# Two post-norm layers on one core: six weight rows instead of four are left to the second token block, the layer norms lose their GpSimd halves, and a layer starts 1024 columns wide

## Chip, cores and metric

The kernel runs on one core of one Trainium2 chip. The metric is the device time of one execution in microseconds (us), the median of three runs. The profile shows one execution of its own, with a span from its first to its last instruction.

## What is computed

A sequence of 256 tokens with 1024 features, in float32, goes through four pre-norm layers (an FFN, a mixer and an FFN each; the mixers are Gated DeltaNet, stick-breaking attention, sparse attention and Gated DeltaNet again), an RMS norm, and two post-norm ("deepnorm") layers. The change is about the two last layers:

```python
for i in range(4):
    x = x + 0.5 * swiglu(rmsnorm(x), ...)          # a0..a3
    x = x + mixer_i(rmsnorm(x))                     # m0 gdn, m1 stick, m2 dsa, m3 gdn
    x = x + 0.5 * swiglu(rmsnorm(x), ...)          # c0..c3
x = rmsnorm(x, final_norm)
for l in range(2):                                  # s0, s1
    h = x @ w_in_2[l]                               # 7696 columns: three branches and their gates
    m = sum(gate_b * (branch_b(h) @ w_branch_2[l, b]) for b in range(3)) @ w_out_2[l]
    x = layer_norm(ALPHA * x + m, ln1_g, ln1_b)     # ALPHA = 4 ** 0.25
    f = relu(x @ w_ff1[l]) ** 2 @ w_ff2[l]          # 4096 wide
    x = layer_norm(ALPHA * x + f, ln2_g, ln2_b)
```

In Gated DeltaNet (`gdn`) each head inverts a unit triangular system of 64 by 64 for each chunk of 64 tokens.

## The kernel before

All activations stay on chip; 503 MB of weights stream through. `fetch` brings 1 MB into a tile `st`; ScalarE (ACT) casts it into the high halves `wh` (L319), and VectorE (DVE) computes the low halves `wl` = `st` - `wh` (L324), so that each product takes three TensorE (PE) matmuls: high by high, high by low, low by high. `wh` and `wl` have WB buffers each. PSUM has eight banks of 512 columns: four with the tag `acc`, two `mm` and two `tr`.

SBUF work tiles come from SLOTS slots of 512 columns. `t()` takes the slot that has been free the longest, `free()` puts one at the end of the line, both while the program is traced. So the number of slots decides which earlier tile a new one takes over from, and whose readers it has to wait for.

The instructions are traced in Python, and a scheduler then gives each engine one fixed order, by priorities (the order of tracing, moved by `rank`) and its own estimates. On the chip each engine follows its order and stops at the first instruction whose inputs or buffers aren't ready.

**The joints in s0 and s1.** A layer norm ends a group of matmuls, `accumulate`, into four `acc` banks (two token blocks t by two halves c of the columns). The last call finishes block 0 over its weight rows and then block 1, so that `deepnorm` can normalize block 0 meanwhile. `deepnorm` forms ALPHA * x + acc (L1316), takes statistics (L1318, L1321), 1/sqrt (`rsqrt1`, L361 to L370), and scales (L1327 on ACT, L1328 on GpSimd, L1329 and L1336 on DVE). For the first half of block 1, ACT copies the bank (L1311) and GpSimd (POOL) does the multiply and the sum (L1312, L1313). `next` puts two of the next weights' `wl` on GpSimd and holds the following four behind the end of block 1's norm, through the list `holds`. Then `xT` transposes x on PE (L418) and splits it (ACT L422, DVE L424): block 0 first; `finish()` does block 1. `cols512(first=True)` multiplies block 0 by 512 columns of weights (L499 to L502) and calls `finish()` in the middle of it. There are three such joints: in s0 from ln1 to its FFN, from s0's ln2 to s1, and in s1 from ln1 to its FFN. An FFN starts with `square` (relu squared: ACT L1592, DVE L1593).

**The solve in `gdn`** (stages m0 and m3, two groups G of heads each: `solve(0)`, `solve(1)`) doubles the solved diagonal blocks in five levels: 32 matmuls of 64 by 64 (L772) into an `acc` bank, a predicated copy on DVE (L773), 32 matmuls (L777), a transpose on DVE (L779) and a copy on ACT (L780), after which the next L772 can start. Between these the scheduler places other PE work, above all projections (`proj_feat`, L588 to L590) into the `mm` banks; each such bank is read out by L644 in `qkv`, into a slot (`c0`).

Of the kernel before, what the change touches and what calls it, by code (L numbers as in the profile page):

```python
# [18 lines left out]
P = 128  # L19
S = 256  # L20
# [5 lines left out]
SLOTS = 57  # L26
ST = 3
WB = 6
# [40 lines left out]
# 16 columns, and zeros up to 128  # L69
# [36 lines left out]
def second_blocks(i, l):  # L106
    w = i["w_in_2"][l]
    z = lambda c: [pack(w[:512, c : c + 512]), pack(w[512:, c : c + 512])]
    out = z(1024) + [pack(padded(w[:, 2048:2064]))]
    for c in (1536, 0, 512, 3088, 3600, 4112, 2064, 2576, 4624, 5136, 5648, 6160, 6672, 7184):  # L110
# [82 lines left out]
# [P, n, S], two blocks of features to a tile  # L193
# [10 lines left out]
class Build:  # L204
# [19 lines left out]
    # loads a set of functions for ScalarE, behind an instruction  # L224
# [6 lines left out]
    # Exp and Ln from one set  # L231
# [3 lines left out]
    # instructions traced here compete as if traced at point p  # L235
# [6 lines left out]
    # a goes behind b on their engine  # L242
# [13 lines left out]
    # a few columns of SBUF  # L256
# [3 lines left out]
    # [P, 512] of PSUM  # L260
# [3 lines left out]
    # up to 512 columns of SBUF, in the slot that has been free the longest  # L264
# [22 lines left out]
    # loads the next block of the weight stream, with x(i) behind each of its n parts  # L287
# [12 lines left out]
    # next block of the weight stream, [P, a, b], as a (h, l) for each of its a rows:  # L300
    # exact float32r halves, w == h + l
# [37 lines left out]
    # y = 1/sqrt(v), elementwise on [P, n]  # L339
# [16 lines left out]
    # y = 1/sqrt(v) for one column: a Newton step with constants for this first guess, then a cubic step  # L356
# [16 lines left out]
    # halves of (x * g)^T, [P (feature), NK, S], of x in blocks of features; g: the stage that has the gain  # L373
# [9 lines left out]
    # sums of x^2 of every token: two columns  # L383
# [15 lines left out]
    # 1/sqrt(mean(x^2) + eps) of every token: two columns, and along the free axis  # L399
# [9 lines left out]
    # halves of x^T of token blocks. The first block is taken as soon as it is there; finish() takes the second.  # L409
# [21 lines left out]
    # r of every token along the free axis, the same on every partition  # L431
# [10 lines left out]
    # acc[t][c] += pairs of feature blocks @ their rows of the next weights;  # L442
    # at the end the blocks of tokens are finished one after the other
    def accumulate(self, acc, pairs, first, last):
        ws = [self.weights(2, 1024) for _ in pairs]
        n = len(pairs)
        order = [(i, a, t, c) for i in range(n) for a in range(2) for t in range(2) for c in range(2)]
        if last:
            self.mark = None
            order = [(i, a, t, c) for t in range(2) for c in range(2) for i in range(n) for a in range(2)]  # L450
        for i, a, t, c in order:
            if last and t and self.mark is None:
                self.mark = self.tc.cur_priority
            (hT, lT), (wh, wl) = pairs[i], ws[i][a]
            q = slice(t * P, t * P + P)
            s = slice(c * 512, c * 512 + 512)
            self.mm3(acc[t][c], hT[:, a, q], lT[:, a, q], wh[:, s], wl[:, s], first and i == 0 and a == 0, last and i == n - 1 and a == 1)
# [27 lines left out]
    # products of both token blocks with the next 512 columns of weights, in step or one after the other  # L485
    # (the first ones of a stage, while the second block of tokens is still on its way)
    def cols512(self, X, banks, first=False):
        XH, XL = X
        w = self.w2()
        mm = self.nc.tensor.matmul  # L490
        if first:
            for t in range(2):
                q = slice(t * P, t * P + P)
                for g in range(0, NK, 4):
                    if (t, g) == (0, 4):
                        self.finish()
                    for k in range(g, g + 4):
                        wh, wl = w[k]
                        mm(banks[t], XH[:, k, q], wh, start=k == 0, stop=False)  # L499
                        mm(banks[t], XH[:, k, q], wl, start=False, stop=False)  # L500
                    for k in range(g, g + 4):
                        mm(banks[t], XL[:, k, q], w[k][0], start=False, stop=k == NK - 1)  # L502
                if t == 0:
                    self.mid = self.tc.cur_priority
            return
# [7 lines left out]
    # x += 0.5 * swiglu(rmsnorm(x))  # L513
# [36 lines left out]
    # x += heads @ w_out, by features  # L550
# [8 lines left out]
    # [128 features, S] products with the next 512 columns of weights, two blocks of features to a bank  # L559
# [16 lines left out]
    # [tok, n] products of a token block  # L576
# [5 lines left out]
    # [128 features, S] products, features f*128.. of the block  # L582
# [9 lines left out]
    # two heads of proj_feat in a bank  # L592
# [8 lines left out]
    def gdn(self, x, st):  # L601
# [33 lines left out]
        # silu of the convolution of a kind (q, k, v) of a group: [feature, 2 heads, tok] twice  # L635
# [30 lines left out]
        # squared norms of the heads of [tok, 4 * 128]  # L666
# [8 lines left out]
        # beta and decay of each token and head  # L675
# [31 lines left out]
        # decay from token j to token i, [i, j] for j <= i  # L707
# [14 lines left out]
        # U = T^T of T = (I - am)^-1, am the strict part of the system, negated (its diagonal is never used); rows scaled: 1/rk T rk  # L722
        def solve(G):
# [38 lines left out]
            # doubling of the diagonal blocks, up to 64: both of them on their half of the partitions  # L762
# [38 lines left out]
        def scan(G):  # L801
# [35 lines left out]
            # scale of the queries: P^-1/2 / norm  # L837
# [19 lines left out]
        # gates and normalizes the heads; their halves, transposed  # L857
# [40 lines left out]
    # halves of a [feature, 2, S] bank  # L898
# [19 lines left out]
    # stick-breaking attention; keys on partitions, queries along the free axis.  # L918
    # z, sp and att hold (key block 0, queries 0..255) and (key block 1, queries 128..255)
# [56 lines left out]
    # rotary embedding of the first r of every group of n columns: [P, groups, n] -> out  # L976
# [16 lines left out]
    # attention weights of a head: (queries 0..127, keys 0..127) and (queries 128..255, keys 0..255);  # L993
    # mask is added to the scores
# [20 lines left out]
    # out [d, S] = the weights p of a head, times its values in two blocks of tokens  # L1015
# [11 lines left out]
    # halves of transposes of [tok, n * 128] columns: [P, n, S], scaled by g along the features  # L1027
# [12 lines left out]
    def dsa(self, x, st):  # L1040
# [6 lines left out]
        # cq 384, k_rope 32, k_idx 64, w_idx 8; and c_kv 256  # L1047
# [19 lines left out]
        # 1/rms of c_q, c_kv and k_idx; c_q and c_kv are scaled by theirs after the products with them  # L1067
# [11 lines left out]
        # cos and sin times 1/rms of c_q: [P, 2, 2, 16] and [P, 2, 2, 8]  # L1079
# [29 lines left out]
        # index keys and queries, [feature, tok]; the keys lie twice on the partitions  # L1109
# [20 lines left out]
        # scores  # L1130
# [22 lines left out]
        # heads: the 96 plain features first, then the 32 rotated ones  # L1153
# [37 lines left out]
        # the largest 64 scores of each query  # L1191
# [32 lines left out]
    # a [1, n] input on every partition, in tiles of 512 columns  # L1224
# [9 lines left out]
    # x * gain * r of all tokens, in blocks of tokens, [t][c]  # L1234
# [16 lines left out]
    # the rotations and the causal mask of the last two stages  # L1251
# [8 lines left out]
    # cos and sin of positions * inv, [P, 2, 16] each  # L1260
# [34 lines left out]
    # the weights of the next stage wait while block t is finished, by instruction z  # L1295
    def next(self, t, z):
        self.holds += [[None] * 2 + ["gpsimd"] * 2, [z] * 4][t]

    # x = layer norm of ALPHA * x + acc, one block of tokens and then the other
    def deepnorm(self, x, acc, gname, bname):  # L1300
# [377 lines left out]
```

## Time and profile before

| | |
|---|---|
| time, median of 3 runs | 3035.79 us (3034.38 to 3035.9) |
| span of the profiled execution | 3030.8 us |
| mean granted clock of TensorE | 0.994 |
| PE busy | 2986.9 us, 99% of the span |
| DVE, ACT, POOL busy | 65%, 51%, 6% |
| waits of PE by the chain of semaphores: largest, L418 for L1336 | 10.0 us in 6 waits |

The profiled execution has no time of its own besides its span; the median run is 5.0 us longer than that span, which is what lies before the first and behind the last instruction. A difference is added to either. PE is busy nearly all the time, so what counts is where it isn't, and where its clock isn't full.

### The profile page before, as it was taken

How to read it: one execution, taken by the hardware profiler on the slowest of the kernel's cores; microseconds unless marked ns; L12 is line 12 of the kernel's file. 1: busy time of each engine (PE TensorE's matmuls, PEld its weight loads, DVE VectorE, ACT ScalarE, POOL GpSimd, SP SyncE). 2: the span in 40 equal slices, each digit the busy share in tenths (PEclk: the TensorE clock that was granted, in tenths of full speed). 3: DMA queues.
4: the chain of work that ended last, by engine and by line, in shares of the span. 5: the costliest groups of instructions: out<-in, count | busy, mean ns of one | idle time of the engine just before them, and what ended most of it. 6: DMA issues, size and time to landing. Idle time of an engine off the chain costs nothing.

```text
span 3030.8 us, 56638 instructions
## 1 busy us (share of the span) xinstructions
PE 2986.9 (99%) x23672; PEld 2843.2 (94%) x23672; DVE 1956.4 (65%) x3013; ACT 1542.2 (51%) x2887; POOL 188.6 (6%) x191
## 2 busy tenths in 40 slices
PE   9999999999999999999999999999999999999998
PEld 9998999999899999879999999999889898889897
DVE  6569865755565565676565598855766756665755
ACT  5455554544554454565454465544554554554553
POOL 1011000000110000210000020000000101000100
PEclk9999999999999999999999999999999999999999
DMA  6442355555445555425555542454455465355453
GB/s 248 181 174 99 112 182 188 185 183 181 153 166 183 181 184 192 153 98 191 186 181 183 172 142 83 175 187 164 164 176 186 172 203 175 139 184 179 174 201 112
DMA packets 73617, 513.07 MB, mean 169 GB/s; under 512 B 8414, under 2 KB 8430, under 8 KB 13456
## 3 DMA queue, kind: packets, MB, share of 16 engines
q1 hardware_dynamic: 70992, 502.50, 46.8%
q0 software_dynamic: 2080, 6.43, 0.8%
q8 instruction: 185, 3.03, 0.4%
q14 instruction: 72, 0.59, 0.1%
q10 hardware_dynamic: 288, 0.52, 0.0%
HBM read 508.37 MB, written 1.05 MB: 168 GB/s over the span
## 4 chain that ended last, share of the span: by engine, by line
PE 54%; DVE 3%; ACT 1%; issue 1%; POOL 0%; DVEq 0%; POOLq 0%; ACTq 0%
PE mm L571 5%; PE mm L573 5%; PE mm L572 5%; PE acc L336 3%; PE acc L335 3%; PE acc L337 3%; PE acc L478 3%; PE acc L477 3%; PE acc L479 3%; PE tr L571 2%; PE tr L573 2%; PE tr L572 2%; PE mm L337 1%; PE mm L335 1%; PE mm L336 1%; PE mm L590 1%
## 5 line engine op out<-in xcount | busy, mean ns | idle before, releaser
L319 ACT CAST wh<-st 128x512 fp32r<-128x512 f32 x1909 | 1093.2, 617 | 1118.8 <-issue 428.6
L324 DVE TENSOR_TENSOR wl<-st,wh 128x1024 fp32r<-128x1024 f32 (+1 forms) x946 | 1155.5, 1228 | 774.3 <-ACT wh L319 771.2
L571 PE MATMUL mm<-s,wh 128*128 128x256 f32 x2240 | 633.5, 283 | 7.1 <-ACT wh L319 7.1
L573 PE MATMUL mm<-s,wl 128*128 128x256 f32 x2240 | 633.1, 283 | 0.1
L572 PE MATMUL mm<-s,wh 128*128 128x256 f32 x2240 | 632.3, 282 | 0.0
L478 PE MATMUL acc<-s,wh 128*128 128x256 f32 x1664 | 468.7, 282 | 0.0
L479 PE MATMUL acc<-s,wl 128*128 128x256 f32 x1664 | 467.5, 282 | 0.0
L477 PE MATMUL acc<-s,wh 128*128 128x256 f32 x1664 | 465.9, 282 | 0.0
L571 PEld LDWEIGHTS mm<-s,wh 128*128 128x128 f32 x2240 | 424.7, 190 | 8.1 <-ACT wh L319 7.1
L572 PEld LDWEIGHTS mm<-s,wh 128*128 128x128 f32 x2240 | 424.6, 190 | 0.7
L573 PEld LDWEIGHTS mm<-s,wl 128*128 128x128 f32 x2240 | 424.1, 189 | 0.3 <-DVE wl L324 0.3
L572 PE MATMUL tr<-s,wh 128*128 128x256 f32 x1280 | 361.6, 282 | 0.0
L571 PE MATMUL tr<-s,wh 128*128 128x256 f32 x1280 | 361.6, 282 | 0.0
L573 PE MATMUL tr<-s,wl 128*128 128x256 f32 x1280 | 360.9, 282 | 0.0
L478 PEld LDWEIGHTS acc<-s,wh 128*128 128x128 f32 x1664 | 314.0, 189 | 1.7 <-DVE s L905 1.3
L479 PEld LDWEIGHTS acc<-s,wl 128*128 128x128 f32 x1664 | 313.4, 189 | 0.0
L477 PEld LDWEIGHTS acc<-s,wh 128*128 128x128 f32 x1664 | 312.6, 189 | 0.1
L572 PEld LDWEIGHTS tr<-s,wh 128*128 128x128 f32 x1280 | 242.1, 189 | 0.0
L571 PEld LDWEIGHTS tr<-s,wh 128*128 128x128 f32 x1280 | 242.0, 189 | 0.0
L573 PEld LDWEIGHTS tr<-s,wl 128*128 128x128 f32 x1280 | 241.8, 189 | 0.0
L335 PE MATMUL acc<-wh,s 128*128 128x512 f32 (+1 forms) x410 | 159.8, 390 | 1.3 <-DVE s L1002 1.0
L337 PE MATMUL acc<-wh,s 128*128 128x512 f32 (+1 forms) x410 | 160.6, 392 | 0.0
(490 smaller groups left out, 4590.4 us busy)
## 6 DMA issues: line engine op xcount, KB each, us to landing
st<-w SPq DMA_DIRECT2D x468, 1024.0 KB, 4.9
st<-w SPq DMA_DIRECT2D x4, 768.0 KB, 4.2
st<-w SPq DMA_DIRECT2D x8, 256.0 KB, 6.0
st<-w SPq DMA_DIRECT2D x4, 512.0 KB, 3.5
s<-s_ln_g POOLq DMA_DIRECT2D x8, 256.0 KB, 3.7
s<-s_ln_b POOLq DMA_DIRECT2D x8, 256.0 KB, 4.5
st<-w SPq DMA_DIRECT2D x2, 976.0 KB, 4.9
s<-x SPq DMA_DIRECT2D x4, 256.0 KB, 5.7
```

The source lines that it names most:

```text
L319: nc.scalar.copy(h[:, o : min(m, o + 512)], st[:, i * b + o : i * b + min(m, o + 512)])
L324: z = e.tensor_tensor(l[:, c], st[:, i * b + c.start : i * b + c.stop], h[:, c].bitcast(F32), ALU.subtract)
L335: mm(out, xh, wh, start=start, stop=False)
L336: mm(out, xh, wl, start=False, stop=False)
L337: mm(out, xl, wh, start=False, stop=stop)
L477: mm(out, wh[:, s], h, start=begin and f == 0, stop=False, skip_group_check=True)
L478: mm(out, wh[:, s], l, start=False, stop=False, skip_group_check=True)
L479: mm(out, wl[:, s], h, start=False, stop=end, skip_group_check=True)
L571: mm(out, wh[:, s], XH[:, k, :], start=k == 0 and f % 2 == 0, stop=False, skip_group_check=True)
L572: mm(out, wh[:, s], XL[:, k, :], start=False, stop=False, skip_group_check=True)
L573: mm(out, wl[:, s], XH[:, k, :], start=False, stop=k == NK - 1, skip_group_check=True)
L590: mm(out, wl[:, s], XH[:, k, :], start=False, stop=k == NK - 1, skip_group_check=True)
```

## The change

The slots go from 57 to 45, the weight buffers from 6 to 9. The last `accumulate` leaves six rows (`apart=6`) of eight to be done block by block, where it was four of four; for that it takes all four pairs of blocks at once (in the FFN the seventh chunk waits for the eighth). In `deepnorm` the first half of block 1 is done on DVE as the others are, `next` goes, and with it the holds: the scheduler places the `wl` of the next weights. A new function `ahead` takes the place of `cols512(first=True)`: the FFN starts with 512 columns as before, s1 with 1024 (banks and `gb`), block 0 first. The weight blocks of s0 and s1 are reordered to suit. Lines that only lose a comment are left out of the diff. Line numbers shift: in `gdn` by two (L772 is now L774, L777 L779, L779 L781, L644 L646), in `deepnorm` by nine (L1316 is L1307, L1318 L1309, L1336 L1327), in `square` L1593 is L1584.

```diff
-SLOTS = 57
+SLOTS = 45
 ST = 3
-WB = 6
+WB = 9
...
-    def accumulate(self, acc, pairs, first, last):
-        ws = [self.weights(2, 1024) for _ in pairs]
-        n = len(pairs)
-        order = [(i, a, t, c) for i in range(n) for a in range(2) for t in range(2) for c in range(2)]
-        if last:
-            self.mark = None
-            order = [(i, a, t, c) for t in range(2) for c in range(2) for i in range(n) for a in range(2)]
-        for i, a, t, c in order:
-            if last and t and self.mark is None:
+    def accumulate(self, acc, pairs, first, last, apart=6):
+        rows = [(z[0][:, a, :], z[1][:, a, :], *w) for z in pairs for a, w in enumerate(self.weights(2, 1024))]
+        n = len(rows)
+        m = n - apart if last else n
+        order = [(i, t, c) for i in range(m) for t in range(2) for c in range(2)]
+        order += [(i, t, c) for t in range(2) for c in range(2) for i in range(m, n)]
+        for z, (i, t, c) in enumerate(order):
+            if last and z == len(order) - 2 * apart:
                 self.mark = self.tc.cur_priority
...
+    def ahead(self, X, pairs):
+        XH, XL = X
+        mm = self.nc.tensor.matmul
+        w = [self.w2() for _ in pairs]
+        end = (0, len(pairs) - 1, 4)
+        for t, i, g in [(t, i, g) for t in range(2) for i in range(len(pairs)) for g in range(0, NK, 4)]:
+            q, out = slice(t * P, t * P + P), pairs[i][t]
+            if (t, i, g) == end:
+                self.finish()
+            for k in range(g, g + 4):
+                wh, wl = w[i][k]
+                mm(out, XH[:, k, q], wh, start=k == 0, stop=False)
+                mm(out, XH[:, k, q], wl, start=False, stop=False)
+            for k in range(g, g + 4):
+                mm(out, XL[:, k, q], w[i][k][0], start=False, stop=k == NK - 1)
...
-    def next(self, t, z):
-        self.holds += [[None] * 2 + ["gpsimd"] * 2, [z] * 4][t]
...
-                if not end and (t, c) == (1, 0):
-                    y = self.t(512)
-                    A.copy(y, acc[t][c])
-                    G_.tensor_scalar(x[t][c], x[t][c], ALPHA, None, ALU.mult)
-                    G_.tensor_tensor(x[t][c], x[t][c], y, ALU.add)
-                    self.free(y)
-                else:
-                    z = V.scalar_tensor_tensor(x[t][c], x[t][c], ALPHA, acc[t][c], ALU.mult, ALU.add)
-                    self.behind(z, None if end else done)
+                z = V.scalar_tensor_tensor(x[t][c], x[t][c], ALPHA, acc[t][c], ALU.mult, ALU.add)
+                self.behind(z, None if end else done)
...
-            self.next(t, done)
...
-        self.cols512(X, banks, not start)
+        gb = [self.bank("acc") for _ in range(2)]
         if start:
+            self.cols512(X, banks)
             ps = self.sums(x)
+            p = self.tc.cur_priority
+            self.cols512(X, gb)
+        else:
+            self.ahead(X, [banks, gb])
...
-        self.cols512(X, b2, True)
+        self.ahead(X, [b2])
...
-            self.accumulate(acc, prev, ch == 0, ch == 7)
+            if ch == 6:
+                held = prev
+            else:
+                self.accumulate(acc, held + prev if ch == 7 else prev, ch == 0, ch == 7)
```

The scheduler's orders show three places. The first is PE in `solve(0)` of m0, the second and third levels of the doubling (L772 and L777; the projections are L588 to L590). Before:

```order
L772 MATMUL acc_2933<-s_361_2804,s_332_2629 64x64 x8
L772 MATMUL acc_2933<-s_361_2804,s_335_2636 64x64 x8
L590 MATMUL mm_3664<-s_267_2280,wl_3585 128x256
L588 MATMUL mm_3664<-s_267_2280,wh_3584 128x256
L589 MATMUL mm_3664<-s_271_2284,wh_3584 128x256
L590 MATMUL mm_3664<-s_267_2280,wl_3585 128x256
L590 MATMUL mm_3603<-s_268_2281,wl_3592 128x256
L588 MATMUL mm_3603<-s_268_2281,wh_3591 128x256
L589 MATMUL mm_3603<-s_272_2285,wh_3591 128x256
L590 MATMUL mm_3603<-s_268_2281,wl_3592 128x256
L588 MATMUL mm_3603<-s_269_2282,wh_3596 128x256
L777 MATMUL acc_2951<-s_383_2893,s_360_2803 64x64 x16
```

Now (L774 and L779 are the solve's; L755 are transposes for `solve(1)`; the three levels after the second stand as bare):

```order
L779 MATMUL acc_2913<-s_382_2892,s_360_2803 64x64 x16
L755 MATMUL tr_3191<-s_357_2742 128x128 x2
L774 MATMUL acc_2933<-s_361_2804,s_332_2629 64x64 x8
L774 MATMUL acc_2933<-s_361_2804,s_335_2636 64x64 x8
L779 MATMUL acc_2951<-s_383_2893,s_360_2803 64x64 x16
L774 MATMUL acc_2971<-s_361_2804,s_332_2629 64x64 x8
L774 MATMUL acc_2971<-s_361_2804,s_335_2636 64x64 x8
L779 MATMUL acc_2989<-s_382_2892,s_360_2803 64x64 x16
```

Nine projections stood between this L772 and its L777, and 21, 8, 15, 10 and 11 in the places that follow; now the first projection stands behind the fifth level's L774. The order of m3 has the same piece.

The second place is DVE in the same stretch, with buffer numbers (`s37_445` is tile 445 in slot 37; `nm` is `s43_383`, which L779 `acc_391` reads). L644, now L646, reads out a projection's bank. Before:

```order
L324 TENSOR_TENSOR wl_454_3585<-st_450_3577,wh_453_3584 128x1024
L352 SCALAR_TENSOR_TENSOR rsy8_371_2830<-rsa8_372_2831,rsj8_370_2829 128x8
L644 TENSOR_TENSOR s37_445_3456<-mm_446_3457,s33_315_2570 128x512
L350 SCALAR_TENSOR_TENSOR rsa8_372_2831<-rsy8_371_2830 128x8
L351 TENSOR_TENSOR rsa8_372_2831<-rsa8_372_2831,nv_362_2806 128x8
```

Now:

```order
L781 STREAM_TRANSPOSE s23_360_2803<-acc_389_2989 128x512
L775 COPY_PREDICATED s43_383_2893<-prm_72,acc_390_3009 128x512
L781 STREAM_TRANSPOSE s23_360_2803<-acc_391_3027 128x512
L646 TENSOR_TENSOR s43_445_3456<-mm_446_3457,s12_315_2570 128x512
L775 COPY_PREDICATED s42_382_2892<-prm_72,acc_392_3047 128x512
L652 SCALAR_TENSOR_TENSOR s42_444_3455<-s43_445_3456,prm_72,s42_444_3455 128x255
```

The read-out of bank `mm_446` stood ahead of the solve's first level; it now takes the slot of a tile of the solve and stands behind the solve's fourth level.

The third place is DVE at the joint in s0 from ln1 to the FFN: the norm of token block 1. Before (behind the last row two L1336 and then `square`'s L1593 follow):

```order
L1318 BN_STATS lnst_27585<-s_3343_25042 128x6
L1321 BN_AGGR lnmv_27593<-lnst_27585 128x2
L1323 TENSOR_SCALAR nmu_27595<-lnmv_27593 128x1
L1324 TENSOR_SCALAR lnmv_27593<-lnmv_27593 128x1
L1329 SCALAR_TENSOR_TENSOR s_3342_25041<-s_3342_25041,lnmv_27593,s_3748_27546 128x512
L361 TENSOR_SCALAR r1i_27598<-lnmv_27593 128x1
L362 TENSOR_SCALAR r1j_27599<-r1i_27598 128x1
L364 TENSOR_SCALAR r1a_27601<-r1j_27599,lnmv_27593 128x1
```

Now (ahead of it stand L1307 and one more `wl`; behind it the rest of `rsqrt1` and two L1327):

```order
L1309 BN_STATS lnst_27585<-s_3343_25042 128x6
L324 TENSOR_TENSOR wl_27754<-st_27746,wh_27753 128x1024
L1312 BN_AGGR lnmv_27590<-lnst_27585 128x2
L324 TENSOR_TENSOR wl_27761<-st_27758,wh_27760 128x1024
L1314 TENSOR_SCALAR nmu_27592<-lnmv_27590 128x1
L1315 TENSOR_SCALAR lnmv_27590<-lnmv_27590 128x1
L1320 SCALAR_TENSOR_TENSOR s_3342_25041<-s_3342_25041,lnmv_27590,s_3748_27546 128x512
L361 TENSOR_SCALAR r1i_27595<-lnmv_27590 128x1
L324 TENSOR_TENSOR wl_27766<-st_27758,wh_27765 128x1024
L362 TENSOR_SCALAR r1j_27596<-r1i_27595 128x1
L1584 SCALAR_TENSOR_TENSOR s_3801_27739<-mm_27646,s_3800_27738 128x512
L324 TENSOR_TENSOR wl_27905<-st_27902,wh_27904 128x1024
```

Five `wl` now stand inside this norm, and `square`'s L1584 (between its neighbours L362 and L364) has moved ahead of the norm's end. On PE the transposes of block 1 stand directly behind the 24 matmuls of block 0.

## Rows read from the trace of the kernel before

**Rows 1.** The page: span, and busy time of each engine.
```profile
span 3030.8 us, 56638 instructions
PE 2986.9 (99%) x23672; PEld 2843.2 (94%) x23672; DVE 1956.4 (65%) x3013; ACT 1542.2 (51%) x2887; POOL 188.6 (6%) x191
```

**Rows 2.** PE's waits: total us, times, longest us.
```profile
PE tr L418 <- DVE s L1336: 10.0, 6, 4.3
PE mm L571 <- ACT wh L319: 7.1, 1, 7.1
```

**Rows 3.** Busy time in two stretches of m0: window, length, each engine, granted clock.
```profile
260.00:320.00 60.00, 59.67 (x945) 54.35 (x944) 51.33 (x118) 27.87 (x57) 6.62 (x8) 1.00 0.23 83
320.00:360.00 40.00, 39.98 (x322) 36.99 (x321) 33.91 (x84) 21.55 (x43) 0.00 (x0) 1.00 0.24 90
```

**Rows 4.** Timeline, all engines, one level of `solve(1)` in m0: start, us, engine, instruction.
```profile
307.79 0.28 PE L777 MATMUL acc<-s,s 64*64 64x64 f32 x4
...
308.12 0.72 DVE L779 STREAM_TRANSPOSE s<-acc 128x512 f32<-128x512 f32 x1 [1.36 <-PE acc L777]
...
308.92 0.59 ACT L780 COPY s<-acc 128x512 f32<-128x512 f32 x1 [4.45 <-DVE s L779]
...
309.41 0.28 PE L589 MATMUL mm<-s,wh 128*128 128x256 f32 x1
...
309.52 0.28 PE L590 MATMUL mm<-s,wl 128*128 128x256 f32 x1
...
309.74 1.15 PE L772 MATMUL acc<-s,s 64*64 64x64 f32 x32
...
310.81 0.38 PE L588 MATMUL mm<-s,wh 128*128 128x256 f32 x1
...
311.00 0.74 DVE L773 COPY_PREDICATED s<-prm,acc 128x512 f32<-128x512 int32 x1 [2.17 <-PE acc L772]
...
311.95 1.15 PE L777 MATMUL acc<-s,s 64*64 64x64 f32 x32
```

**Rows 5.** PE alone in four stretches: window, length, PE busy, granted clock, DMA.
```profile
1325.90:1329.80 3.90, 1.92 (x9) 1.00 0.10 40
1329.80:1333.20 3.40, 3.40 (x15) 0.51 0.64 198
...
2381.65:2384.60 2.95, 2.95 (x9) 0.51 0.00 0
2571.80:2575.70 3.90, 3.87 (x11) 0.50 0.74 271
```

**Rows 6.** Timeline of PE at the joint in s0, with the idle time before.
```profile
2378.89 0.63 PE L418 MATMUL tr<-ident,s 128*128 128x128 f32 x4 [0.59 <-DVE s L1336]
...
2381.65 1.09 PE L418 MATMUL tr<-ident,s 128*128 128x128 f32 x4 [1.89 <-DVE s L1336]
...
2384.62 0.39 PE L500 MATMUL mm<-wl,s 128*128 128x512 f32 x1
...
2385.08 0.40 PE L500 MATMUL mm<-wl,s 128*128 128x512 f32 x1
```

**Rows 7.** Timeline of DVE at the same joint.
```profile
2377.55 3.95 DVE L1336 SCALAR_TENSOR_TENSOR s<-s,r1z,s 128x512 f32<-128x512 f32 x2
...
2384.13 0.68 DVE L1318 BATCH_NORM_STATS2 lnst<-s 128x6 f32<-128x512 f32 x1
...
2388.00 1.42 DVE L1336 SCALAR_TENSOR_TENSOR s<-s,r1z,s 128x512 f32<-128x512 f32 x2
2389.87 0.69 DVE L1593 SCALAR_TENSOR_TENSOR s<-mm,s 128x512 f32<-128x512 f32 x1 [0.46 <-ACT s L1592]
```

**Rows 8.** Timeline of POOL at the same joint.
```profile
2378.15 5.58 POOL L324 TENSOR_TENSOR wl<-st,wh 128x1024 fp32r<-128x1024 f32 x2
```

**Rows 9.** Timeline of PE at the joint from s0 to s1.
```profile
2571.83 1.12 PE L418 MATMUL tr<-ident,s 128*128 128x128 f32 x4 [4.32 <-DVE s L1336]
```

**Rows 10.** The page's group of DVE's `wl`: busy us, mean ns, idle before.
```profile
L324 DVE TENSOR_TENSOR wl<-st,wh 128x1024 fp32r<-128x1024 f32 (+1 forms) x946 | 1155.5, 1228 | 774.3 <-ACT wh L319 771.2
```

More of the change, by code (lines that the diff above doesn't have):

```diff
@@ L108, in second_blocks @@
     z = lambda c: [pack(w[:512, c : c + 512]), pack(w[512:, c : c + 512])]
-    out = z(1024) + [pack(padded(w[:, 2048:2064]))]
-    for c in (1536, 0, 512, 3088, 3600, 4112, 2064, 2576, 4624, 5136, 5648, 6160, 6672, 7184):
+    out = z(1024) + z(1536) + [pack(padded(w[:, 2048:2064]))]
+    for c in (0, 512, 3088, 3600, 4112, 2064, 2576, 4624, 5136, 5648, 6160, 6672, 7184):
         out += z(c)
@@ L440, in along @@
         return rb
-    def accumulate(self, acc, pairs, first, last):
-        ws = [self.weights(2, 1024) for _ in pairs]
-        n = len(pairs)
-        order = [(i, a, t, c) for i in range(n) for a in range(2) for t in range(2) for c in range(2)]
-        if last:
-            self.mark = None
-            order = [(i, a, t, c) for t in range(2) for c in range(2) for i in range(n) for a in range(2)]
-        for i, a, t, c in order:
-            if last and t and self.mark is None:
+    def accumulate(self, acc, pairs, first, last, apart=6):
[6 more added lines that the diff above has]
+            if last and z == len(order) - 2 * apart:
                 self.mark = self.tc.cur_priority
-            (hT, lT), (wh, wl) = pairs[i], ws[i][a]
+            hT, lT, wh, wl = rows[i]
             q = slice(t * P, t * P + P)
             s = slice(c * 512, c * 512 + 512)
-            self.mm3(acc[t][c], hT[:, a, q], lT[:, a, q], wh[:, s], wl[:, s], first and i == 0 and a == 0, last and i == n - 1 and a == 1)
+            self.mm3(acc[t][c], hT[:, q], lT[:, q], wh[:, s], wl[:, s], first and i == 0, last and i == n - 1)
         self.free(*pairs)
@@ L483, in accs, with cols512 @@
         return [[self.bank("acc") for c in range(2)] for t in range(2)]
-    def cols512(self, X, banks, first=False):
+    def cols512(self, X, banks):
         XH, XL = X
         w = self.w2()
[L490 to L505, printed above, removed]
         for k in range(NK):
@@ L511, in cols512 @@
                 self.mm3(banks[t], XH[:, k, q], XL[:, k, q], *w[k], k == 0, k == NK - 1)
+    def ahead(self, X, pairs):
[13 more added lines that the diff above has]
+                mm(out, XL[:, k, q], w[i][k][0], start=False, stop=k == NK - 1)
+            if (t, i, g) == end:
+                self.mid = self.tc.cur_priority
     def ffn(self, x, st):
@@ L1372, in second @@
         banks = [self.bank("mm") for _ in range(2)]
-        self.cols512(X, banks, not start)
+        gb = [self.bank("acc") for _ in range(2)]
         cos, sin = self.cosp, self.sinp
         if start:
+            self.cols512(X, banks)
             ps = self.sums(x)
+            p = self.tc.cur_priority
+            self.cols512(X, gb)
+        else:
+            self.ahead(X, [banks, gb])
         lr = self.bank("acc")
         self.proj_feat(*X, self.weights(8, P), lr[:, :S], 0)
-        p = self.tc.cur_priority
-        gb = [self.bank("acc") for _ in range(2)]
-        self.cols512(X, gb)
         if start:
@@ L1580, in second @@
         acc = self.accs()
-        for j in range(2):
-            self.accumulate(acc, pairs[2 * j : 2 * j + 2], j == 0, j == 1)
+        self.accumulate(acc, pairs, True, True)
         x = self.deepnorm(x, acc, f"{st}_ln1_g", f"{st}_ln1_b")
```

## The prediction

> **What bounds the kernel now.** I read the busy times first [rows 1]: PE works for 2986.9 of 3030.8 us, so no more than 44 us of idle time can be won, and every microsecond that PE is newly kept waiting is lost. Next the waits of PE [rows 2]: the largest is the transposes of the joints waiting for the layer norm, 10.0 us in six waits; the next, 7.1 us for the first weights, is the start of the program. No later wait for `wh` or `wl` of any size is in that view, so nine weight buffers have nothing to win over six. Then the granted clock [rows 5]: where PE pauses, it falls from its upper level (2.4 GHz, shown as 1.00) to the lower (1.2 GHz, shown as 0.5), and the matmuls that follow run at half speed, so a pause costs more than its own length. Last, stretches of m0 [rows 3]: there PE is busy for 59.67 of 60 and 39.98 of 40 us. The serial chain of the solve costs nothing there now, because projections stand in its gaps.
>
> **The joints, first block.** The two L1336 of block 0 take 3.95 us where those of block 1 take 1.42 [rows 7]: the slow pair runs while GpSimd computes two `wl` [rows 8]. The joint in s0 loses 0.59 + 1.89 us of PE [rows 6] and half of the 2.95 us that follow at clock 0.51 [rows 5], 3.9 us. The joint to s1 is the longest wait, 4.32 us [rows 9], with some 0.57 more before it (what the total of ten leaves to six waits in three like patterns), and half of 3.9 us at clock 0.50 [rows 5], 6.8 us. The joint in s1 repeats the first, 4.0 us. Together 14.7 us. The change takes the `wl` off GpSimd, and puts 23 matmuls between the end of block 0 and its first transposes. At 0.23 us each (two matmuls from 2384.62 to 2385.08 [rows 6]) this is 5.3 us of cover, against a chain that I work out below at 4.6 us behind the first half's statistics plus 0.7 for L1307, 5.3 us. I leave 0.4 us at each joint for this wait.
>
> **The joints, second block.** Here cover is lost. Before, block 1's norm runs without a `wl` in it: from its last L1318 at 2384.13 to its first L1336 at 2388.00 are 3.9 us, and half of the 1.42 us of the pair makes 4.6 [rows 7]. Now the order has L1307 (about 0.7, as the equally wide L1593 [rows 7]) and five `wl` of 1.23 us [rows 10] in this chain, which can't start before block 1's last matmul of `accumulate`: 4.6 + 0.7 + 6.1 = 11.4 us. In the two FFN joints `square`'s L1584 stands in it too, another 0.7: 12.1 us. All of it is on DVE in fixed order, and PE's transposes are queued behind 24 matmuls, with all later PE work behind them: cover 24 x 0.233 = 5.6 us, so PE waits 6.5 us, and the half clock behind it costs 1.7 (between the two stretches above). An FFN joint then costs 0.4 + 6.5 + 1.7 = 8.6 us, 4.6 more than before. In the joint to s1, 48 matmuls (1024 columns) cover 11.2 us of 11.4; with the first block's rest and one late weight I put 1.2 us, 5.6 less. The joints: 2 x 4.6 - 5.6 = +3.6 us. The bounds: a `wl` could be cheaper only if it stood elsewhere, and it doesn't, but if the chain of 12.1 overlapped `accumulate` entirely, the joints would cost about nothing, -14.5; if every `wl` waits for its cast on ACT in turn, one or two us more at each, +8.
>
> **The solve in `gdn`.** The 45 slots give the read-out of bank `mm_446` the slot of a tile of the solve, so it stands on DVE behind the fourth level; both `mm` banks stay full, and PE's order has no projection for three levels. Of one level [rows 4]: from the end of L777 (308.00, four matmuls behind 307.79) DVE's L779 and ACT's L780 lead to L772 at 309.74, 1.74 us; its 32 matmuls are through at 310.81; L773 leads to L777 at 311.95, 1.14 us. Before, projections filled these gaps; the six that are bare now leave PE idle for 3 x (1.74 + 1.14) = 8.6 us. The gap ahead of them holds two transposes of 0.12, which leaves 1.5. In it DVE also has two `wl` of 1.23 us in front of the transpose L781, against 1.2 us that it would wait for L779 anyway, so it comes some 1.3 us later. Against that, each entry of projections cost about 0.1 us as PE changed over and 0.1 as it changed back (0.22 from 309.52 to 309.74 against 0.11 from 309.41, and 0.38 for the L588 behind it against 0.28 [rows 4]): six fewer, 1.2 us. A stage loses 8.6 + 1.5 + 1.3 - 1.2 = 10.2 us, if the projections, which are no fewer, find no other hole: the 40 us behind have 0.02 us idle [rows 3]. As bounds I keep 7.4 (the six gaps less the changes) and 11.4.
>
> In such a level two groups of matmuls stand between two pauses. The nearest row for what the clock does then is the stretch from 1325.90 in m2: PE worked in pieces with pauses between them, 1.92 of 3.90 us, and then came 3.40 us at clock 0.51 [rows 5]. At half clock 32 matmuls of 64 columns take about 1 us more (1.07 doubled; no row has them). If the clock falls in the second bare level, four or five such groups, and the projections that follow for one stretch of 3 to 4 us, are slow: 4.5 + 1.6, some 6 us a stage. The bounds are nothing, and 10 if it falls at once and stays for two stretches. I take 6, since PE did there what it will do here.
>
> The Trainium skill, "TensorE: Matmul & The Clock Gate", section "What's actually happening", says that the array's clock is halved once it has been idle, and full again once it has been busy. Read strictly, with gaps of 1.74 us at most between groups of matmuls, it would stay full here: the sum would be without the 6 us, rival B's. The row from 1325.90, where the clock fell behind work in pieces, speaks against that reading.
>
> m0 and m3 have the same piece of order, so 2 x (10.2 + 6) = +32.4 us.
>
> **The rest.** The order in m2 changes where DVE is the one waited for; I find moves both ways and take 0, with 3 us either way. Six rows instead of four and the held chunk issue the same matmuls. The end of the program has no next stage. L1311 to L1313 leave ACT and GpSimd, which wait there anyway, and add 0.7 us on DVE, counted above.
>
> **The sum.** +32.4 + 3.6 = +36 us on the profiled span: 3030.8 + 36 = 3066.8; with the 5.0 us outside it, 3071.8, and the same on the median, 3035.8 + 36. I say 3071 us.
>
> **Rivals.**
> - A, not slower: the projections, moved back, fill later holes, so the bare levels cost little net. Then the joints alone remain, 3039 us, and any gain in m2 or at a joint puts it below the old time; it decides if the two stages together lose under 3 us. Nearly no holes are in the stretch behind [rows 3], but the work that follows is also moved, and new holes may come where they can use them.
> - B, the clock stays full in the levels: 3035.8 + 20.4 + 3.6 = 3060.
> - C, the second block's waits don't arise at the FFN joints: the joints give 14.5, 3035.8 + 32.4 - 14.5 = 3054. It would need DVE to have this chain done beside `accumulate`; the order and L1307's need of the last bank speak against it.
> - D, slots that come free later keep other tiles waiting too (the branches of s0 and s1 have the same 45), or the clock stays low through `solve(1)`: 15 us more, 3087.
>
> **Chances.** The forecast 0.56, A 0.10, B 0.18, C 0.05, D 0.11. Within 0.2% (6 us) is about what a measurement of this kernel can tell from no change. A splits into 0.06 within that and 0.04 faster; all the others are slower: 0.90. The range of 3049 to 3087 takes in B and C with some microseconds of m2, and D up to its price; it leaves out A and D's upper half.
>
> **What would show it.** In the profile after: in m0 and m3 gaps of 1.1 and 1.7 us between L774 and L779 over three levels, a clock of 0.5 there, and PE's idle time up by 20 us in the two stages. At the joints, L1327 pairs of 1.42 us throughout, no long wait for block 0, and in the two FFN joints a wait of L418 of 5 to 7 us for block 1, with 1 us or less at the joint to s1. It would be wrong if PE's gaps in the solve are filled, or if the order on DVE in the joints runs ahead of PE's 24 matmuls.

## The result: 1.1% slower, and where the time went

The changed kernel takes 3068.52 us (median of four runs, 3065.81 to 3070.26), the kernel before 3035.85 beside it: a ratio of 1.0111, 95% interval 1.0098 to 1.0124. The forecast was 3071. The profiled execution has a span of 3064.1 us, 33.3 more than that of before, and a mean granted clock of 0.989. Its own time is 3065.81 us: 1.7 us lie outside the span, as in every other run, and not the 5.0 that were taken for it ahead of the prediction. The rest of the 5.0 is the difference between two executions of the kernel before, and falls out of every difference below.

The page of the changed kernel, against [rows 1]:

```profile
span 3064.1 us, 56713 instructions
PE 2995.0 (98%) x23672; PEld 2851.2 (93%) x23672; DVE 1962.0 (64%) x3022; ACT 1547.8 (51%) x2884; POOL 175.9 (6%) x179
```

PE runs the same number of matmuls. It is idle 25 us more (69 against 44), and its own busy time is 8 us longer; matmuls at the lower clock, shown below, are in that. The waits of PE in the changed kernel, against [rows 2] (columns: total us, times, longest):

```profile
PE tr L418 <- DVE s L1327: 12.2, 5, 5.7
PE acc L774 <- ACT s L782: 12.1, 8, 1.6
PE mm L573 <- ACT wh L319: 7.3, 1, 7.3
PE acc L779 <- DVE s L775: 5.9, 6, 1.2
PE tr L437 <- DVE rr L436: 3.5, 2, 2.6
```

Three new things are in it: the solve's own chain (L774 and L779, 18.0 us together, which had no such rows before), another pattern of waits at the joints with a like sum (12.2 us against 10.0), and a wait of L437 that the prediction doesn't have.

To see which stage pays, take the end of the last write of x by each stage's FFN or mixer. From a0's end to m0's: 183.6 us before, 195.8 now, so m0 costs 12.2 us more. From a3's end to m3's: 183.5 and 196.9 us, 13.4 more. m2 is unchanged (105.8 and 105.7). PE alone in m0 before and now, and in m3 before and now (window, length, PE busy, clock):

```profile
205.30:388.90 183.60, 182.51 (x1895) 1.00 0.33 122
205.80:401.60 195.80, 184.89 (x1888) 0.97 0.31 109
1747.60:1931.10 183.50, 182.38 (x1894) 1.00 0.35 122
1764.40:1961.30 196.90, 185.93 (x1888) 0.96 0.31 108
```

In each of them PE is idle 9.8 us more, and busy some 2.4 and 3.5 us more. For the joints, take the last matmul of each closing `accumulate`: between these the three stretches go from 187.7 to 190.1, from 266.2 to 260.0 and from 186.7 to 189.1 us: +2.4, -6.2 and +2.4. Between c3's end and the first of these ends are 3.9 us more, at the start of s0. What is left, 33.3 - 25.6 + 1.4 - 3.9 = 5.2 us, is spread over the other stages in parts of -0.5 to +1.6.

**The solve after.** The timeline of PE in `solve(0)` of m0, L774 and L779 alone, with the idle time before each in brackets:

```profile
266.12 0.71 PE L755 MATMUL tr<-s 128*128 128x128 f32 x4
268.28 1.15 PE L774 MATMUL acc<-s,s 64*64 64x64 f32 x32 [1.45 <-ACT s L782]
270.58 1.15 PE L779 MATMUL acc<-s,s 64*64 64x64 f32 x32 [1.15 <-DVE s L775]
273.32 1.15 PE L774 MATMUL acc<-s,s 64*64 64x64 f32 x32 [1.60 <-ACT s L782]
275.37 1.98 PE L779 MATMUL acc<-s,s 64*64 64x64 f32 x32 [0.90 <-DVE s L775]
278.83 1.97 PE L774 MATMUL acc<-s,s 64*64 64x64 f32 x32 [1.49 <-ACT s L782]
281.70 1.97 PE L779 MATMUL acc<-s,s 64*64 64x64 f32 x32 [0.90 <-DVE s L775]
285.16 1.97 PE L774 MATMUL acc<-s,s 64*64 64x64 f32 x32 [1.49 <-ACT s L782]
...
288.91 1.15 PE L779 MATMUL acc<-s,s 64*64 64x64 f32 x32
```

Seven gaps, 9.0 us of idle time. From the fourth group on, 32 matmuls take 1.97 instead of 1.15 us. The windows of PE show the clock in m0 and then in m3 (length, PE busy, clock):

```profile
266.80:275.00 8.20, 3.48 (x97) 1.00 0.32 124
275.00:288.60 13.60, 9.35 (x135) 0.50 0.00 1
1825.50:1831.50 6.00, 2.30 (x64) 1.00 0.45 168
1831.50:1848.50 17.00, 11.73 (x168) 0.50 0.00 1
```

From 258 to 266.8 PE has no pause. Then come 8.2 us of pieces with pauses of 1.15 to 1.60 us, and behind them the clock is at its lower level for 13.6 us. In m3 it falls earlier, after 6 us of such pieces and with the third group, and stays low for 17 us.

**The joints after.** The timeline of PE at the joint in s0, against [rows 6], and at the joint to s1, against [rows 9]:

```profile
2410.76 0.63 PE L418 MATMUL tr<-ident,s 128*128 128x128 f32 x4 [0.20 <-DVE s L1327]
2411.46 0.60 PE L418 MATMUL tr<-ident,s 128*128 128x128 f32 x4
...
2426.07 1.94 PE L418 MATMUL tr<-ident,s 128*128 128x128 f32 x8 [5.70 <-DVE s L1327]
...
2616.61 1.29 PE L418 MATMUL tr<-ident,s 128*128 128x128 f32 x8 [0.43 <-DVE s L1327]
```

Block 0 is waited for 0.2 us instead of 2.5. Block 1, not waited for before, keeps PE 5.7 us in s0; at the joint to s1, behind 1024 columns, 0.4 us. DVE at the joint in s0, against [rows 7]:

```profile
2414.89 0.69 DVE L1307 SCALAR_TENSOR_TENSOR s<-s,acc 128x512 f32<-128x512 f32 x1
2415.49 1.22 DVE L324 TENSOR_TENSOR wl<-st,wh 128x1024 fp32r<-128x1024 f32 x1
2416.63 0.69 DVE L1309 BATCH_NORM_STATS2 lnst<-s 128x6 f32<-128x512 f32 x1
...
2421.61 0.68 DVE L1584 SCALAR_TENSOR_TENSOR s<-mm,s 128x512 f32<-128x512 f32 x1
2422.20 0.27 DVE L364 TENSOR_SCALAR r1a<-r1j,lnmv 128x1 f32<-128x1 f32 x1
2422.39 1.45 DVE L324 TENSOR_TENSOR wl<-st,wh 128x1024 fp32r<-128x1024 f32 x1
...
2425.18 1.41 DVE L1327 SCALAR_TENSOR_TENSOR s<-s,r1z,s 128x512 f32<-128x512 f32 x2
```

No wait stands ahead of any step of DVE in this stretch: the norm of block 1 takes from 2414.89 to 2425.89 for its first half, five `wl` and the square among its steps. The L1327 pair is at 1.41 us.

### The profile page after: what moved, and what is told of

The parts are those of the page before. It is cut to its first block, busy times and chain, and to the rows that moved or that the text cites. A ratio compares the mean times of both kernels' runs of the same rounds, so it can differ in the third digit from the quotient of the medians.

```text
span 3064.1 us, 56713 instructions
## 1 busy us (share of the span) xinstructions
PE 2995.0 (98%) x23672; PEld 2851.2 (93%) x23672; DVE 1962.0 (64%) x3022; ACT 1547.8 (51%) x2884; POOL 175.9 (6%) x179
## 4 chain that ended last, share of the span: by engine, by line
PE 63%; DVE 5%; issue 1%; ACT 1%; DMA 0%; POOL 0%; DVEq 0%; ACTq 0%; SPq 0%; POOLq 0%
PE mm L573 6%; PE mm L575 6%; PE mm L574 6%; PE acc L477 4%; PE acc L476 4%; PE acc L478 4%; PE tr L573 3%; PE tr L575 3%; PE tr L574 3%; PE acc L337 3%; PE acc L336 3%; PE acc L335 2%; DVE wl L324 1%; PE mm L335 1%; PE mm L337 1%
## 5 line engine op out<-in xcount | busy, mean ns | idle before, releaser
L324 DVE TENSOR_TENSOR wl<-st,wh 128x1024 fp32r<-128x1024 f32 (+1 forms) x952 | 1170.9, 1237 | 771.3 <-ACT wh L319 769.6
L319 ACT CAST wh<-st 128x512 fp32r<-128x512 f32 x1909 | 1092.1, 617 | 1083.0 <-issue 461.9
L573 PE MATMUL mm<-s,wh 128*128 128x256 f32 x2240 | 633.6, 283 | 7.3 <-ACT wh L319 7.3
L574 PE MATMUL mm<-s,wh 128*128 128x256 f32 x2240 | 632.0, 282 | 0.0
L335 PE MATMUL acc<-wh,s 128*128 128x512 f32 (+1 forms) x394 | 155.3, 394 | 2.5 <-DVE s L1004 2.2
L590 PE MATMUL mm<-s,wh 128*128 128x256 f32 x544 | 156.8, 288 | 0.1
```

Source lines behind the costliest of these rows:

```text
L319: nc.scalar.copy(h[:, o : min(m, o + 512)], st[:, i * b + o : i * b + min(m, o + 512)])
L324: z = e.tensor_tensor(l[:, c], st[:, i * b + c.start : i * b + c.stop], h[:, c].bitcast(F32), ALU.subtract)
L335: mm(out, xh, wh, start=start, stop=False)
L573: mm(out, wh[:, s], XH[:, k, :], start=k == 0 and f % 2 == 0, stop=False, skip_group_check=True)
L574: mm(out, wh[:, s], XL[:, k, :], start=False, stop=False, skip_group_check=True)
L590: mm(out, wh[:, s], XH[:, k, :], start=k == 0, stop=False, skip_group_check=True)
```

## Experiments

The theory: the fewer slots let the read-out of a projection wait for the solve, so PE's order has bare levels; their idle time and the lower clock behind them cost 12 to 14 us a stage. At the joints, `wl` and the square inside block 1's norm replace what GpSimd cost before.

**1. The slots alone.**

```diff
-SLOTS = 57          # on the kernel before
+SLOTS = 45
```

> The kernel before with 45 slots and nothing else changed (6 weight buffers, GpSimd halves and holds as before). Its order on PE has the same bare levels in the solve as the changed kernel. Theory (the slots alone cause the loss in gdn): m0 and m3 take 12 to 14 us more each, the joints stay as before, 3036 + 26 = 3062 us. Rival (nine weight buffers or the freed schedule are needed for the loss): within 5 us of 3036. Rival A of the prediction (later holes take the projections in): also near 3036.

Measured: 3060.89 us, a ratio of 1.0082 (1.0067 to 1.0097), 25 us more than before. The stages m0 and m3 take 14.1 and 15.1 us more. PE's waits in this kernel (line numbers of before):

```profile
PE acc L772 <- ACT s L780: 11.9, 8, 1.6
PE tr L418 <- DVE s L1336: 9.3, 8, 1.9
...
PE acc L777 <- DVE s L773: 5.9, 6, 1.2
```

The same 17.8 us of waits in the solve as in the changed kernel, from one number. Nine buffers and the norms have no part in it, and no later hole takes the projections in: rival A falls. The joints were expected as before. Two of them are, but the stretch with the joint to s1 is 3.7 us shorter, and PE's longest wait for a norm is 1.9 us where it was 4.3 [rows 9], with nothing changed but the slots. Why is not shown by any run.

**2. More slots in the changed kernel.**

```diff
-SLOTS = 45
+SLOTS = 49
-WB = 9
+WB = 8
```

> The changed kernel with 49 slots and 8 weight buffers in place of 45 and 9, the same SBUF in sum. PE's order has projections in every level of the solve again. Theory (the slot that the read-out takes decides): the 26 us of m0 and m3 go, 3068.5 - 26 = 3043 us, with the waits for block 1 at the FFN joints left. Rival (the fewer slots cost elsewhere, or the clock and the bare levels were not the cause): above 3055.

Measured: 3046.46 us, 1.0037 (1.0024 to 1.0050): 22 us won back of 26. m0 and m3 are still 5.7 and 4.9 us over before. The order of this kernel has one bare level left, the last but one group of `solve(1)`, and PE's timeline there shows it:

```profile
315.15 1.15 PE L774 MATMUL acc<-s,s 64*64 64x64 f32 x32 [0.69 <-ACT s L782]
317.56 1.15 PE L779 MATMUL acc<-s,s 64*64 64x64 f32 x32 [1.26 <-DVE s L775]
319.18 0.41 PE L790 MATMUL acc<-ident,s 64*64 64x64 f32 x4 [0.47 <-ACT s L787]
```

PE's window from there (length, PE busy, clock):

```profile
316.00:330.00 14.00, 12.27 (x112) 0.65 0.43 152
```

Idle time of 2.4 us here is followed by a clock of 0.65 on average over 14 us. The expectation said that all levels are filled, and overlooked the one in the second solve.

**3. The clock by itself.** Needless matmuls in the bare gaps; their results are overwritten.

```diff
                 ps = b8()
+                fill(ps, 10 if G == 0 and s >= 8 else 0)
...
                 pu = b8()
+                fill(pu, 6 if G == 0 and 4 <= s <= 16 else 0)
...
+            def fill(out, n):
+                for k in range(n):
+                    mm(out.rearrange("p h n -> p (h n)")[:, 0:S], X[0][:, k % NK, 0:P], X[0][:, k % NK, :], start=True, stop=True)
```

> The changed kernel with 48 needless matmuls of 256 columns in the first solve of m0 and m3, into the banks that the next L774 or L779 overwrite, placed by the scheduler in the bare gaps (8, 13, 8, 13 and 6 of them). They compute nothing that is used, so the bare levels stay as long as their chain. Theory (half of the loss beyond the idle time is the clock, which falls because PE pauses): no stretch at 0.5 in the solve, levels 5.0 us apart throughout, 3 to 4 us less for each stage, 3068.5 - 7 = 3061 us. Rival (the clock isn't what lengthens the levels, or the chain alone sets them): 3068 or more.

Measured: 3057.43 us, 1.0076 (1.0061 to 1.0091), so 11 us less than the changed kernel, with some 6 us of uncertainty; m0 is 10.3 and m3 8.8 us over before, 6.5 less in sum than in the changed kernel. PE at the same place (L779 and L785 are the solve's here):

```profile
268.91 1.15 PE L779 MATMUL acc<-s,s 64*64 64x64 f32 x32 [1.45 <-ACT s L788]
271.23 1.15 PE L785 MATMUL acc<-s,s 64*64 64x64 f32 x32
274.06 1.15 PE L779 MATMUL acc<-s,s 64*64 64x64 f32 x32
276.29 1.15 PE L785 MATMUL acc<-s,s 64*64 64x64 f32 x32
279.11 1.15 PE L779 MATMUL acc<-s,s 64*64 64x64 f32 x32
...
283.81 1.15 PE L779 MATMUL acc<-s,s 64*64 64x64 f32 x32 [1.49 <-ACT s L788]
...
286.02 1.15 PE L785 MATMUL acc<-s,s 64*64 64x64 f32 x32
```

The window that stood at 0.50 in the changed kernel:

```profile
275.00:288.60 13.60, 12.11 (x217) 1.00 0.01 2
```

The clock stays at 1.00 and the groups at 1.15 us. From 268.91 to the same group three levels on (283.81) are 14.9 us, against 16.9 without the needless work; to the last group shown, behind the first projections, they are 17.1 against 20.6. More matmuls, and less time: the clock's part is shown, and B, in which it stays up, falls.

**4. The weights held behind block 1's norm.**

```diff
                     done = V.scalar_tensor_tensor(z, z, rs, b[c], ALU.mult, ALU.add)
+        if not end:
+            self.holds += [None] * (8 if "ln2" in gname else 4) + [done] * 6
```

> The changed kernel with the weights of the next stage held: the wl that the first block's columns need run at once (four, or eight at the joint to s1), the following six behind the end of block 1's norm. No GpSimd. Theory (the five wl and the square in the norm of block 1 make the wait): L418's two waits of 5.7 us go down to under 1 us each and the clock stays up behind them, 14 us less, 3068.5 - 14 = 3054 us. Rival (the held wl are late for what follows and PE waits for them there): L324 or L319 appear in PE's waits with several us, within 4 us of 3068.

Measured: 3052.70 us, 1.0054 (1.0037 to 1.0071), 15.8 us less than the changed kernel, again with some 6 us of uncertainty. In the order the square also fell behind the norm's end, so this run doesn't tell the five `wl` from it. PE's wait for the norms:

```profile
PE tr L418 <- DVE s L1327: 0.4, 2, 0.2
```

From 12.2 us to 0.4, with no half clock at the joints. The held `wl` were late for nobody.

**5. The start of s0.**

```diff
         if start:
             self.cols512(X, banks)
             ps = self.sums(x)
-            p = self.tc.cur_priority
-            self.cols512(X, gb)
...
         self.proj_feat(*X, self.weights(8, P), lr[:, :S], 0)
         if start:
+            p = self.tc.cur_priority
+            self.cols512(X, gb)
```

The weight blocks of s0 are put into the same order.

> The changed kernel with s0's start in the order of before: the 16 columns of lr ahead of the second 512 columns, and the norm behind them. Theory (the final norm's transposes L437 wait because lr no longer lies ahead of them): the wait of 2.6 us and the half clock behind it go, 4 us less, 3064.5 us. Rival (the wait only moves to the products that need lr): no change, 3068.5 us.

Measured: 3063.87 us, 1.0091 (1.0076 to 1.0106), 4.6 us less than the changed kernel, which is within the uncertainty of two such runs; in the profile the stretch from c3's end to the first joint is 4.5 us shorter than in the changed kernel, and no other stage is by more than 0.2. In the changed kernel's timeline of PE:

```profile
2169.32 0.46 PE L437 MATMUL tr<-ident,rr 128*128 128x128 f32 x1 [2.61 <-DVE rr L436]
```

With lr ahead, the row (L439 there) is one wait of 0.9 us:

```profile
PE tr L439 <- DVE rr L438: 0.9, 1, 0.9
```

**6. The three together, with 49 slots and 8 buffers.** The edits of 2, 4 and 5.

> Slots 49 with 8 weight buffers, the held wl and lr ahead of the norm, together. If the three are separate losses they add: 3068.5 - 22 - 15.8 - 4.6 = 3026 us, 10 us faster than before. Rival (the joints and the solve share a cause, such as DVE's load): above 3032.

Measured: 3032.26 us over ten runs, 0.9992 (0.9982 to 1.0001): no difference from before that can be told. The three gains do not add: 6 us are missing. By the ends of `accumulate` the joints win 12.5 us on before, where experiment 4 wins 16.2, and of PE's waits 2.8 us in five are again for the norms; m0 and m3 stay 4.2 and 1.6 us over before, and c3 2.2.

**7. The same with 53 slots, paid for with the third stream buffer.**

```diff
-SLOTS = 49
+SLOTS = 53
-ST = 3
+ST = 2
```

> As the kernel with 49 slots, held wl and lr ahead, with 53 slots, which two stream buffers st in place of three make room for. Its order has projections in all levels of both solves. Theory (what is left in gdn with 49 slots, 5 us a stage, is the one bare level of the second solve and the half clock behind it): m0 and m3 at the time of before, 3026 - 10 = 3016 us. Rival (two stream buffers make the weights late): waits of PE for L319 or L324 all over the span, above 3030.

Measured: 3055.31 us, 1.0067 (1.0052 to 1.0082): a miss by 39 us. The solve was as expected (m0 2.3 and m3 1.4 us over before), but every other stage from c0 to the first joint is 1.6 to 5.5 us longer. The largest wait of PE:

```profile
PE acc L439 <- DVE rr L438: 12.4, 7, 2.3
```

The rival named waits for L319 or L324. It is the RMS norms that come late, in seven waits of up to 2.3 us; I did not trace the chain that leads to them. The edit changes the slots too; experiment 9 has 53 slots with three stream buffers and waits of 1.9 us in all for these norms, which points to the stream buffers without showing it.

**8. The kernel before without GpSimd in the norms.** Four rows apart and 512 columns ahead as before.

```diff
-        self.holds += [[None] * 2 + ["gpsimd"] * 2, [z] * 4][t]
+        self.holds += [[None] * 4, [z] * 4][t]
...
-                if not end and (t, c) == (1, 0):
-                    y = self.t(512)
-                    A.copy(y, acc[t][c])
-                    G_.tensor_scalar(x[t][c], x[t][c], ALPHA, None, ALU.mult)
-                    G_.tensor_tensor(x[t][c], x[t][c], y, ALU.add)
-                    self.free(y)
```

> The kernel before with 57 slots and 6 weight buffers, four rows for each block and 512 columns ahead, without GpSimd: the first half of block 1 on DVE, and the four wl of the next weights on DVE at once, the other four held. Theory: the L1336 pair of block 0 is back at 1.42 us and the wait for block 0 under 1 us; but with six buffers two of the four wl come into block 1's norm, with the square, so PE waits some 3 us for block 1 and runs 3.4 us at half clock: about 5 us at each joint, 3036 + 1 at the FFN joints and -2 at the joint to s1, 3034 to 3038 us. Rival (GpSimd isn't what blocks DVE): the pair of block 0 stays at 3.9 us or more, above 3045.

Measured: 3032.72 us over ten runs, 0.9992 (0.9983 to 1.0001): 1.3 us under the expected range, and no difference from before that can be told. All L1336 of the kernel before (count, then ns least/median/most, first and last start):

```profile
L1336 DVE SCALAR_TENSOR_TENSOR s<-s,r1z,s x14: 740/806/5285, 2377.6 to 3025.9; 128x512 f32<-128x512 f32 x14
```

The same instruction, L1329, in this kernel:

```profile
L1329 DVE SCALAR_TENSOR_TENSOR s<-s,r1z,s x14: 740/748/854, 2380.8 to 3026.9; 128x512 f32<-128x512 f32 x14
```

What left GpSimd are the two `wl` and the multiply and sum of block 1, and the longest falls from 5.3 us to 0.85: it is GpSimd's work that held DVE. That it is the `wl` is read from the times ([rows 7] and [rows 8]); this run does not part them from the rest. The gain goes into two `wl` now in block 1's norm and waits of PE up to 2.4 us for it, as expected, and at each joint into a wait of 1.0 us for a `wl`, which was not.

**9. The same with 7 buffers and 53 slots, the square behind the norm.**

```diff
-SLOTS = 57
+SLOTS = 53
-WB = 6
+WB = 7
...
+            self.behind(z, self.normed)          # z: the square's DVE step
```

> The kernel before without GpSimd in the norms (four rows apart, 512 columns ahead), with 53 slots and 7 weight buffers, and the square kept behind the end of the norm. Its order has projections in all levels of the solves, one wl instead of two in block 1's norm and no square there. Theory (with the solve's levels filled, the joints are all that there is to win, and what stands in block 1's norm sets them): the waits for L418 fall from 10.0 us in sum to 2 or 3, with no half clock at the joints, 3036 - 10 = 3026 us. Rival (the gain at the joints is given back, as with 6 buffers): 3032 to 3036 us, with a wait of 1.5 us or more for block 1 at each joint.

Measured: 3031.14 us over eleven runs, 0.9988 (0.9979 to 0.9997): 3 us better than before, where 10 were expected. It is the lowest ratio here, but its interval overlaps those of experiments 6 and 8. At each joint PE still waits 2.0 us for block 1, as at the one in s0:

```profile
2390.79 1.29 PE L418 MATMUL tr<-ident,s 128*128 128x128 f32 x8 [1.99 <-DVE s L1329]
```

One `wl` is left in the norm, and the four L424 of block 0 stand ahead of its statistics; I had not counted the latter. That is the rival's 1.5 us or more. By the ends of `accumulate` the joints win 4.6 us; m1 and m2 are 1.7 and 2.4 us longer than before, which may in part be the spread of executions (in experiment 8, with the slots and buffers of before, m2 was 1.5 us longer).

**10. The changed kernel once more.**

> The changed kernel once more, as a control of what one profile says of single stages. If the 5 us by which the stages other than m0, m3, s0 and s1 came out longer in its first profile are the change's doing, the same stages are longer by the same amounts again (a2, a3 and c3 by 1.1 to 1.6 us). If they are the spread of executions, they change by a microsecond either way, while m0 and m3 stay at 12 to 14 us more. Time 3066 to 3071 us.

Measured: 3068.27 us. m0 and m3 are 13.1 and 13.3 us over before, and a2, a3 and c3 1.3, 1.5 and 1.1, as in the first profile (1.4, 1.6 and 1.1). So the scattered 5 us belong to the change. The kernel before was profiled once, but experiment 8, the same up to s0, repeats its c0, c1, a2 and c3 within 0.1 us (a3 is 0.6 longer there). The FFN joints are 3.5 and 3.1 us dearer in this second profile, where the first had 2.4: single stretches are good to about a microsecond.

## Why the prediction was right, point by point

**The solve, right, and 6.8 us too large.** The bare levels, their length and their place came out as said. The idle time was put at 11.4 us a stage ahead of the six changes of work; over each stage PE is idle 9.8 us more, 9.0 of it in the seven gaps of m0. The two `wl` ahead of L781 cost next to nothing (a gap of 1.45 us, where I had 1.5 + 1.3): PE's L755 and DVE's steps overlapped with them. The clock was put at 6 us a stage. PE is busy 2.4 and 3.5 us longer; with the 1.2 us put down to the changes of work, an estimate that no run tested, the clock's part is 3.6 in m0 and 4.7 in m3, and in m0 the needless matmuls won 3.5 of the same stretch. The clock falls with the fourth group (the third in m3), and the slow groups take 0.8 us more, not 1, while the gaps between them shrink (1.15 to 0.90). 2 x 16.2 = 32.4 was forecast, 25.6 measured.

**The first block, right.** L1327 at 1.41 us in all joints, 0.2 us of wait where I left 0.4.

**The second block, right in kind, 5.0 us too large.** The FFN joints: a wait of 6.5 us was forecast and is 5.7, because DVE steps that follow one another overlap: the chain's row durations add up to 12.1 us, but the steps start 1.13 to 1.14 us apart where a `wl` is shown with 1.21 or 1.22, and the chain is 11.0 us long. The FFN joints came out 2.4 us dearer each, not 4.6: the shorter waits (1.0 us) and 1.4 instead of 1.7 us for the clock, half of what PE worked at the lower level, are 1.3 of these 2.2, and the rest is not traced. The joint to s1 won 6.2, where 5.6 were forecast; experiments 1 and 8 win 3.7 and 3.6 of it in the same stretch without the 1024 columns. Together -1.4 instead of +3.6: the change does win time at the joints, less than it could.

**What was missing: the start of s0.** The step "The rest" has no term for it. The order of lr and gb in s0 was visible in the diff, with the norm's rank in front of gb; lr's matmuls no longer lie ahead of the norm's transposes. It costs 3.9 us in the profile and 4.6 by experiment 5. The same step has nothing for the scattered 5 us. These two (9.1 us) make up for most of what the solve and the joints were given too much (11.8), so that the sum is nearer (36 against 32.7) than its terms is luck.

**The rivals.** A fell by experiment 1, B by 3. C needed the second block's waits not to arise; they did, and experiment 4 shows that they were avoidable. Of D, the later slots: no long new wait at the branches of s0 and s1 shows in PE's waits.

What the Trainium skill says in "TensorE: Matmul & The Clock Gate", section "What's actually happening", read strictly, was B, 3060 us. The trace differs: here the clock fell without one pause longer than 1.6 us (in m0 8.2 us of pieces at 1.00, then 13.6 us at 0.50), and needless matmuls in the pauses kept it up.

**Open.** What makes c0, c1, a2, a3 and c3 0.7 to 1.6 us longer each, in both profiles, is not settled. It is neither a wait nor the clock in c0, where PE is busy throughout at a clock of 1.00:

```profile
401.60:593.80 192.20, 192.20 (x1616) 1.00 0.52 182
```

In experiment 1 only a3 of them was more than half a microsecond longer (1.4), which speaks for the nine buffers or the moved code in the others, and for the slots in a3. Why the norms are late in experiment 7, why the slots alone shorten the joint to s1, and how much of experiment 4 is the square's, also stay open.

## What to carry to other kernels

Memory that is taken from work tiles is paid for where a new tile inherits a slot from a tile that is still in use: look in the new order for stretches where the busy engine has lost the work that filled its waits, also in stages that the diff never names. In this kernel nine microseconds of short pauses cost some four more through the clock. Behind a norm on the critical path hold every step that nobody needs yet, and count what PE has to do until it must have the result.

## What the runs showed of the hardware

- 32 matmuls of 64 by 64 by 64 took 1.15 us at the upper clock and 1.97 at the lower, 1.7 times as long: I had doubled them. The lower clock came behind pieces of such matmuls with pauses of no more than 1.6 us. Needless matmuls in the pauses made the same chain 2.0 us shorter over three levels.
- A DVE instruction of 128 x 512 with two SBUF inputs took 5.29 us at most beside GpSimd's `wl`, and 0.85 at most in experiment 8, where the `wl` and the multiply and sum of block 1 are off GpSimd.
